# Head norms of a hybrid decoder trunk: the factor of a block by an addition and a power on GpSimd instead of five steps on ScalarE and VectorE

## The chip, the cores and the metric

The kernel runs on one core of one Trainium2 chip. The metric is the device time of one execution in microseconds. Of the kernel before there are three runs: median 1257.32 us, from 1256.88 to 1257.96. One further execution was taken with the hardware profiler; the views in this document come from it.

In the views PE is TensorE (matrix products), PEld its weight loads, DVE is VectorE, ACT is ScalarE, POOL is GpSimd and SP is SyncE, which only issues transfers. L520 is line 520 of the kernel before. Names such as s_tq are the program's tiles, with their numbers left out.

## What is computed

A trunk of two decoder layers on 512 tokens of width 1024, in float32. Layer A has sparse attention with 12 heads and memory attention with 4; layer B has dilated attention with 3 × 8 heads and memory attention with 4. Each layer ends in an MLP with a squared ReLU. Every query and key head of 64 numbers is normalised before the rotary step:

```python
def rmsnorm(x, g):
    x32 = x.astype(jnp.float32)
    y = x32 * lax.rsqrt(jnp.mean(x32 * x32, axis=-1, keepdims=True) + EPS)
    return (y * g.astype(jnp.float32)).astype(x.dtype)
...
    q = rope(rmsnorm(split_heads(q, NSA_HEADS), q_norm), pos).reshape(B, G, R, S, D)
...
    q = rope(rmsnorm(q, q_norm[:, None, None, :]), jnp.arange(S))
...
    q = rmsnorm(split_heads(q, MEM_HEADS), q_norm)
    k = rmsnorm(split_heads(k, MEM_HEADS), k_norm)
```

The scores are scaled by 64 to the power −1/2. The factor of a head is one over the root of its mean square.

## The kernel before, in words

Products of full width are made of three products of rounded halves: each float32 operand is split into a rounded high part and a low part (`wsplit` L263 and L265 for weights, `part` and `split` for activations), and `mm3` (L270 to L272) adds high × high, high × low and low × high in one PSUM bank. So every weight tile of 128 rows costs one copy on ScalarE (L263) and one subtraction on VectorE or GpSimd (L265).

The 512 tokens are four blocks of 128 rows. A projection (`proj`, L310) runs over the blocks, and in each over eight slices of the width; when a block's bank is full, a function `evac` empties it. For projections with heads it does this:

- VectorE multiplies the bank with the gains of the heads into a tile `tq` (L967 and L968 in layer A, L1487 in layer B, L632 for the memory's queries).
- `normf` (L513) makes the factor of each of the block's heads. ScalarE squares the bank (L518). VectorE sums the squares by head (L520). ScalarE then takes the logarithm of the mean square (L522), an exponential of minus half of it with the logarithm of KN in its bias (L523), and a square (L524). VectorE makes one Newton step of the result: sum plus 64 EPS times the square (L526), minus 1.5, times the first guess (L527). The sign and the constant KN are made good in the gains, which `setup2` multiplies once (L447 to L450).
- `rope` (L530) turns the heads, four steps on GpSimd (L537 to L540; VectorE takes blocks 0 and 2 of the first projection).
- `q_out` (L753) multiplies with the factor on GpSimd (L759; L1443 for the keys of layer B), splits the result into halves (L710 on ScalarE, L711 on VectorE), and, some steps of the projection later, lets TensorE transpose it (L768, L778).

`normf` is called 45 times: 12 blocks of `proj_a` and 16 of `proj_b` with six heads each, 8 of `mem_q` and 4 of `mem_out` with four, 4 of `evac_k` with eight, and once for the 96 compressed keys. Its tiles come from small rings of buffers: the sums from tag r4 with two, the three ScalarE results from r5 with two, the factors from r6 with three.

Between the projections' steps stands the attention of earlier heads: scores on TensorE, their maximum on VectorE, exponentials on ScalarE (L226), a scaling on GpSimd (`pscale`, L735), transposes (L1104, L1098, L1622), products with the values (`pair`, L747). Generators and written ratios (RA, RB, RC, DELAY, DX) say how the steps of projections, attention and side work are mixed in the program's text; the Tile framework, called with `schedule_with_timeline_sim=True`, then sets the order of each engine by a timeline that it simulates, and puts in the semaphores. Each engine works off its own queue in that order. GpSimd's queue also issues transfers that add in DRAM (L1191).

The time line of the profiled execution: projections and attention of layer A up to about 300 us, its output projection and MLP to about 670, layer B's keys, queries and attention to about 900, its output projection and MLP to the end. No head norm runs in the MLPs.

Of the kernel before, what the change touches and what calls it, by code (L numbers as in the profile page):

```python
# [10 lines left out]
AF = mybir.ActivationFunctionType  # L11
ALU = mybir.AluOpType
AX = mybir.AxisListType

P = 128
# [4 lines left out]
HD = 64  # L20
EPS = 1e-6
# [5 lines left out]

GR = ["aq", "mq0", "mq1", "bq0", "bq1", "bq2", "ak1", "ak2", "ak0", "mk0", "mk1", "kk", "b2k", "b2v"]
NQ, NK = 6, 12

KN = float(np.sqrt(0.5 / HD))


def bcast(ap, dim, n):

# [145 lines left out]
class K:  # L181
    def __init__(self, ctx, tc, ins, out):
# [13 lines left out]
        self.lab = "s"  # L196

    BUFS = dict(
        act=12, st=3, w=4, qk=8, pt4=4, p2=6, raw=2, tmp=4, sq=1, rb=1, tq=2, qki=2, ki=2, x=8, r1=1, r2=1, r3=1, r4=2, r5=2, r6=3, r7=2, nm=6, su=5, cr=6, c1=2, c2=2, nb=4,
        cs=2, stt=4, vcb=1, ab=1,  # L200
    )

# [234 lines left out]
    def setup2(self):  # L437

        nc = self.nc
        self.on1 = self.c("on1", [P, 1])  # L440
        nc.vector.memset(self.on1, 1.0)
        self.x = [None] * KT
        self.idr = self.c("idr", [P, P], F32R)
        nc.vector.tensor_copy(self.idr, self.idf)
        self.cm = self.c("cm", [P, P], F32R)
        nc.vector.tensor_copy(self.cm, self.cm0)
        for a, z, g in ((0, NQ, -(HD**-0.5) / KN), (NQ, NK, -1.0 / KN)):  # L447
            nc.vector.tensor_scalar(
                out=self.gr[:, a:z], in0=self.gr[:, a:z], scalar1=g, scalar2=None, op0=ALU.mult
            )  # L450
        self.eps = self.c("eps", [P, 3])
        for j, y in enumerate((EPS, HD * EPS, float(np.log(KN)))):
            nc.vector.memset(self.eps[:, j : j + 1], y)

    def setup_b(self):
# [57 lines left out]
    def normf(self, raw, nh, e):  # L513

        nc = self.nc
        p = raw.shape[0]
        sq = self.t("p2" if nh > 6 else "sq", [p, nh, HD])
        nc.scalar.activation(sq.rearrange("p h d -> p (h d)"), raw, AF.Square)  # L518
        ss = self.t("r4", [p, nh])
        nc.vector.tensor_reduce(out=ss, in_=sq, axis=AX.X, op=ALU.add)  # L520
        y = self.t("r5", [p, 3, nh])
        nc.scalar.activation(y[:, 0], ss, AF.Ln, scale=1.0 / HD, bias=e[:, 0:1])  # L522
        nc.scalar.activation(y[:, 1], y[:, 0], AF.Exp, scale=-0.5, bias=self.eps[0:p, 2:3])  # L523
        nc.scalar.activation(y[:, 2], y[:, 1], AF.Square)  # L524
        f = self.t("r6", [p, nh])
        nc.vector.scalar_tensor_tensor(out=f, in0=ss, scalar=e[:, 1:2], in1=y[:, 2], op0=ALU.add, op1=ALU.mult)  # L526
        nc.vector.scalar_tensor_tensor(out=f, in0=f, scalar=-1.5, in1=y[:, 1], op0=ALU.add, op1=ALU.mult)  # L527
        return f

    def rope(self, G, cs, e=None):  # L530
# [1316 lines left out]
```

## Time and profile before

| what | value |
|---|---|
| median of three runs | 1257.32 us (1256.88 to 1257.96) |
| span of the profiled execution | 1254.7 us |
| granted TensorE clock | 1.000 |
| instructions | 18245 |
| bytes moved by transfers | 215.36 MB, 172 GB/s in the mean |
| ScalarE's L522, L523, L524 together | 36.8 us in 135 instructions |
| VectorE's L526, L527 together | 34.5 us in 90 instructions |

The profiled execution's own time is its span, first to last instruction; what lies around it in a run shows in the difference to the median, 2.6 us. Busy time is the time in which an engine had at least one instruction under way; TensorE's matmuls are pipelined and their ends are modelled, so short gaps between them do not show. A row of the groups reads: line, engine, operation, output from input, shape, count, busy time and mean duration in ns of one, idle time of the engine just before them and what ended it. A row of waits reads: engine, tile and line that waited, what it waited for, us in total, times, longest.

### The profile page before, as it was taken

Reading aid. Unit: us, or ns where it says so; the run is one execution under the profiler, and the core shown is the slowest. Engines: PE = TensorE matmul, PEld = TensorE weight load, DVE = VectorE, ACT = ScalarE, POOL = GpSimd, SP = SyncE. Lnnn points to the kernel's source line nnn. Section 1 sums busy time; section 2 is a strip of 40 time slices with the busy share of each in tenths; the row PEclk is TensorE's granted clock in tenths of the full one; section 3 lists DMA queues with packets and bytes.
Section 4 is the critical chain, followed back from the end, with each engine's and each line's share of the span. In section 5 each row is a group of like instructions: output and inputs, shape, how many; then the busy total and the mean of one; then the engine's idle time right before and its main releaser. Section 6 shows DMA issues by size and latency. Waiting matters only on the chain.

```text
span 1254.7 us, 18245 instructions
## 1 busy us (share of the span) xinstructions
PE 1234.1 (98%) x6419; PEld 1018.3 (81%) x6419; DVE 831.1 (66%) x1476; ACT 744.1 (59%) x1643; POOL 341.9 (27%) x452
## 2 busy tenths in 40 slices
PE   9999999999999999999999999999999999999998
PEld 7768877787788888888888899987788888888887
DVE  6857685664576557475599477787767756557466
ACT  6835678783575454554657468778666445364462
POOL 4536874730040000000003687541232000000000
PEclk9999999999999999999999999999999999999999
DMA  7531233342497796986965431110369689697634
GB/s 267 201 106 51 94 102 124 77 111 69 160 278 227 250 257 210 276 244 203 294 205 173 137 91 47 58 39 25 113 185 306 210 267 251 204 291 225 171 104 165
DMA packets 62219, 215.36 MB, mean 172 GB/s; under 512 B 6928, under 2 KB 15312, under 8 KB 61616
## 3 DMA queue, kind: packets, MB, share of 16 engines
q1 hardware_dynamic: 50656, 143.69, 34.8%
q0 software_dynamic: 9728, 35.87, 14.7%
q10 hardware_dynamic: 1744, 34.63, 7.3%
q8 instruction: 51, 0.84, 0.3%
q14 instruction: 40, 0.33, 0.1%
HBM read 208.83 MB, written 72.35 MB: 224 GB/s over the span
## 4 chain that ended last, share of the span: by engine, by line
PE 76%; ACT 4%; DVE 4%; issue 1%; POOL 1%; DMA 0%; ACTq 0%; POOLq 0%; DVEq 0%
PE s_ps L270 13%; PE s_ps L271 13%; PE s_ps L272 13%; PE s_acc L270 5%; PE s_acc L272 5%; PE s_acc L271 5%; PE s_pt L270 3%; PE s_pt L272 3%; PE s_pt L271 3%; PE s_po L747 3%; ACT s_p L226 1%; PE s_ps L1582 1%; PE s_pt L1104 1%; PE s_ps L1069 1%; DVE s_w L265 1%
## 5 line engine op out<-in xcount | busy, mean ns | idle before, releaser
L265 DVE TENSOR_TENSOR s_w<-s_st,s_w 128x1024 fp32r<-128x1024 f32 (+3 forms) x254 | 293.6, 1160 | 250.3 <-ACT s_w L263 249.9
L263 ACT ACTIVATE s_w<-s_st 128x1024 fp32r<-128x1024 f32 (+4 forms) x260 | 251.6, 970 | 203.1 <-PE s_pt L272 58.0
L270 PE MATMUL s_ps<-s_act,s_w 128*128 128x512 f32 x560 | 218.5, 392 | 0.4 <-DVE s_x L1170 0.3
L271 PE MATMUL s_ps<-s_act,s_w 128*128 128x512 f32 x560 | 218.4, 390 | 0.0
L272 PE MATMUL s_ps<-s_act,s_w 128*128 128x512 f32 x560 | 218.1, 390 | 0.0
L1191 POOL DMA_DIRECT2D sum<-sum x16 | 14.2, 887 | 431.9 <-ACT s_p L226 431.9
L271 PEld LDWEIGHTS s_ps<-s_act,s_w 128*128 128x128 f32 x560 | 105.2, 188 | 22.5 <-issue 0.8
L270 PEld LDWEIGHTS s_ps<-s_act,s_w 128*128 128x128 f32 x560 | 105.0, 188 | 22.5 <-DVE s_x L1170 0.8
L272 PEld LDWEIGHTS s_ps<-s_act,s_w 128*128 128x128 f32 x560 | 105.2, 188 | 21.9
L270 PE MATMUL s_acc<-s_w,s_act 128*128 128x512 f32 (+3 forms) x288 | 101.2, 356 | 2.9 <-ACT s_sq L518 1.9
L271 PE MATMUL s_acc<-s_w,s_act 128*128 128x512 f32 (+3 forms) x288 | 101.1, 353 | 0.5 <-DVE s_w L265 0.5
L272 PE MATMUL s_acc<-s_w,s_act 128*128 128x512 f32 (+3 forms) x288 | 99.4, 350 | 0.0
L226 ACT ACTIVATE s_p<-s_ps 128x512 f32<-128x512 f32 x64 | 38.1, 595 | 95.0 <-PE s_ps L272 92.3
L735 POOL TENSOR_SCALAR s_p<-s_p,s_cr,s_ab 128x128 f32<-128x128 f32 (+3 forms) x96 | 61.7, 667 | 58.0 <-DVE s_cr L1080 34.8
L226 ACT ACTIVATE s_p<-s_ps,s_nm 128x256 f32<-128x256 f32 (+3 forms) x128 | 65.6, 527 | 14.1 <-DVE s_nm L726 5.0
L270 PEld LDWEIGHTS s_acc<-s_w,s_act 128*128 128x128 f32 x288 | 54.2, 188 | 9.4 <-ACT s_sq L518 3.1
L743 ACT ACTIVATE s_pt<-s_pt 128x512 f32<-128x512 f32 (+2 forms) x99 | 52.2, 532 | 14.7 <-PE s_pt L1104 5.5
L305 ACT ACTIVATE s_qk<-s_p 128x256 fp32r<-128x256 f32 (+1 forms) x96 | 46.9, 488 | 21.2 <-DVE s_p L1201 19.3
L271 PEld LDWEIGHTS s_acc<-s_w,s_act 128*128 128x128 f32 x288 | 54.3, 188 | 5.2 <-DVE s_w L265 0.9
L272 PEld LDWEIGHTS s_acc<-s_w,s_act 128*128 128x128 f32 x288 | 54.2, 189 | 4.0
L308 DVE TENSOR_TENSOR s_qk<-s_p,s_qk 128x256 fp32r<-128x256 f32 (+1 forms) x96 | 50.9, 530 | 0.0
L271 PE MATMUL s_acc<-s_w,s_qk 128*128 128x512 f32 x128 | 49.9, 390 | 0.0
(335 smaller groups left out, 2833.9 us busy)
## 6 DMA issues: line engine op xcount, KB each, us to landing
s_st<-in_w_up_dram SPq DMA_DIRECT2D x64, 512.0 KB, 4.3
s_st<-sum SPq DMA_DIRECT2D x64, 512.0 KB, 6.0
s_st<-in_w_db_dram SPq DMA_DIRECT2D x48, 512.0 KB, 4.4
sum<-in_w_db_dram POOLq DMA_DIRECT2D x16, 1024.0 KB, 14.1
sum<-sum POOLq DMA_DIRECT2D x16, 1024.0 KB, 12.0
s_st<-in_w_bq_dram SPq DMA_DIRECT2D x16, 384.0 KB, 3.2
s_st<-in_w_ag_dram SPq DMA_DIRECT2D x11, 512.0 KB, 3.6
s_w<-in_w_c_dram SPq DMA_DIRECT2D x8, 512.0 KB, 4.6
```

Of the source, the lines that this page charges most:

```text
L226: return lambda *a, **k: self.marks.append(f(*a, **k))
L263: nc.scalar.activation(w[:, 0], st, AF.Copy)
L265: e.tensor_tensor(out=w[:, 1], in0=st, in1=w[:, 0], op=ALU.subtract)
L270: mm(ps, lh[0], rh[0], start=start, stop=False, skip_group_check=again)
L271: mm(ps, lh[0], rh[1], start=False, stop=False, skip_group_check=again)
L272: mm(ps, lh[1], rh[0], start=False, stop=stop, skip_group_check=again)
L305: nc.scalar.activation(dst[:, 0], src, AF.Copy)
L308: nc.vector.tensor_tensor(out=dst[:, 1], in0=src, in1=dst[:, 0], op=ALU.subtract)
L735: self.nc.gpsimd.tensor_scalar(out=p, in0=p, scalar1=c, scalar2=g, op0=ALU.mult, op1=ALU.mult)
L743: self.turned = self.nc.scalar.activation(dst, src, AF.Copy)
L747: i = self.nc.tensor.matmul(*a, **k)
L1191: self.behind(self.nc.gpsimd.dma_start(t[o], x, accum_op=ALU.add, max_dma_last_dim=4096))
```

## The change

The factor is made from the sum of squares directly. GpSimd adds 64 EPS (times the block's mean square, as before) to the sums in place, and then raises them to the power that a constant tile holds in every element, −0.5. The three ScalarE steps, the two VectorE steps, the tag r5 and KN are gone. Since the factor is now one over the root of the sum, and no longer scaled by KN with a minus sign, the gains of the keys (columns NQ to NK of `gr`) are multiplied by 8 in `setup2`, and those of the queries by nothing: the 1/8 of the scores and the 8 of the norm cancel. The squares (L518), the sums (L520) and everything behind the factor stay as they are.

```diff
-KN = float(np.sqrt(0.5 / HD))
...
-        act=12, st=3, w=4, qk=8, pt4=4, p2=6, raw=2, tmp=4, sq=1, rb=1, tq=2, qki=2, ki=2, x=8, r1=1, r2=1, r3=1, r4=2, r5=2, r6=3, r7=2, nm=6, su=5, cr=6, c1=2, c2=2, nb=4,
+        act=12, st=3, w=4, qk=8, pt4=4, p2=6, raw=2, tmp=4, sq=1, rb=1, tq=2, qki=2, ki=2, x=8, r1=1, r2=1, r3=1, r4=2, r6=3, r7=2, nm=6, su=5, cr=6, c1=2, c2=2, nb=4,
...
-        for a, z, g in ((0, NQ, -(HD**-0.5) / KN), (NQ, NK, -1.0 / KN)):
-            nc.vector.tensor_scalar(
-                out=self.gr[:, a:z], in0=self.gr[:, a:z], scalar1=g, scalar2=None, op0=ALU.mult
-            )
-        self.eps = self.c("eps", [P, 3])
-        for j, y in enumerate((EPS, HD * EPS, float(np.log(KN)))):
+        nc.vector.tensor_scalar(
+            out=self.gr[:, NQ:NK], in0=self.gr[:, NQ:NK], scalar1=HD**0.5, scalar2=None, op0=ALU.mult
+        )
+        self.half = self.c("half", [P, 8])
+        nc.vector.memset(self.half, -0.5)
+        self.eps = self.c("eps", [P, 2])
+        for j, y in enumerate((EPS, HD * EPS)):
             nc.vector.memset(self.eps[:, j : j + 1], y)
...
         nc.vector.tensor_reduce(out=ss, in_=sq, axis=AX.X, op=ALU.add)
-        y = self.t("r5", [p, 3, nh])
-        nc.scalar.activation(y[:, 0], ss, AF.Ln, scale=1.0 / HD, bias=e[:, 0:1])
-        nc.scalar.activation(y[:, 1], y[:, 0], AF.Exp, scale=-0.5, bias=self.eps[0:p, 2:3])
-        nc.scalar.activation(y[:, 2], y[:, 1], AF.Square)
+        nc.gpsimd.tensor_scalar(out=ss, in0=ss, scalar1=e[:, 1:2], scalar2=None, op0=ALU.add)
         f = self.t("r6", [p, nh])
-        nc.vector.scalar_tensor_tensor(out=f, in0=ss, scalar=e[:, 1:2], in1=y[:, 2], op0=ALU.add, op1=ALU.mult)
-        nc.vector.scalar_tensor_tensor(out=f, in0=f, scalar=-1.5, in1=y[:, 1], op0=ALU.add, op1=ALU.mult)
+        nc.gpsimd.tensor_tensor(out=f, in0=ss, in1=self.half[0:p, 0:nh], op=ALU.pow)
         return f
```

## The prediction, made before the result

> **What bounds the kernel now.** I read the page's first part, then busy time by stretch, then the rows of the lines that change, and then what VectorE and GpSimd do around them.
>
> ```profile
> span 1254.7 us, 18245 instructions
> PE 1234.1 (98%) x6419; PEld 1018.3 (81%) x6419; DVE 831.1 (66%) x1476; ACT 744.1 (59%) x1643; POOL 341.9 (27%) x452
> ```
>
> TensorE is idle for 1254.7 − 1234.1 = 20.6 us of the span. Work taken off ScalarE or VectorE pays only where it closes such a gap, and GpSimd at 27% seems to have room. But these are averages. The next view takes six stretches in which head norms run; the view after it counts the norms in them by L527, the last step of each.
>
> ```profile
> 20.00:60.00 40.00, 37.59 (x204) 32.74 (x202) 29.53 (x73) 26.95 (x84) 24.48 (x24) 1.00 0.57 197
> 108.00:142.00 34.00, 34.00 (x204) 28.52 (x203) 26.86 (x59) 21.86 (x64) 30.99 (x46) 1.00 0.21 67
> 161.00:184.00 23.00, 22.13 (x178) 18.71 (x177) 17.59 (x44) 17.39 (x53) 20.92 (x27) 1.00 0.35 112
> 189.00:224.00 35.00, 32.86 (x261) 27.59 (x260) 21.65 (x61) 30.74 (x99) 18.13 (x28) 1.00 0.34 114
> 718.00:760.00 42.00, 39.63 (x246) 37.50 (x245) 32.62 (x56) 26.71 (x77) 34.05 (x36) 1.00 0.33 100
> 803.00:862.00 59.00, 56.72 (x440) 49.59 (x440) 46.47 (x110) 47.34 (x164) 26.92 (x32) 1.00 0.10 30
> ```
>
> ```profile
> 108.00:142.00 34.00, 3.06 (x4) 1.00 0.21 67
> 161.00:184.00 23.00, 1.02 (x2) 1.00 0.35 112
> 718.00:760.00 42.00, 3.82 (x7) 1.00 0.33 100
> ```
>
> The columns of the first are length, then busy time of PE, PEld, DVE, ACT and POOL. PE's gaps are 2.41, 0, 0.87, 2.14, 2.37 and 2.28, together 10.1 us: that is all that this change can win here, 0.8% of the time. And GpSimd is not idle where it counts: 30.99 of 34, 20.92 of 23, 34.05 of 42.
>
> What PE waits for in 718 to 760 us:
>
> ```profile
> PE s_acc L270 <- ACT s_sq L518: 1.5, 3, 0.9
> PE s_pt L768 <- DVE s_qki L711: 0.4, 1, 0.4
> PE s_acc L271 <- DVE s_w L265: 0.3, 1, 0.3
> ```
>
> All three are ScalarE or VectorE arriving late, 2.2 of the 2.37 us. None is the norm's own result: the squares (L518) empty a PSUM bank, and they stand in ScalarE's queue behind other work.
>
> **What is removed.** Each of 45 norms loses five instructions:
>
> ```profile
> L523 ACT ACTIVATE s_r<-s_r,eps x45: 281/298/393, 37.6 to 856.6; 128x6 f32<-128x6 f32 x28, 128x4 f32<-128x4 f32 x12, 128x8 f32<-128x8 f32 x4, 96x1 f32<-96x1 f32 x1
> L524 ACT ACTIVATE s_r<-s_r x45: 188/208/261, 37.9 to 857.6; 128x6 f32<-128x6 f32 x28, 128x4 f32<-128x4 f32 x12, 128x8 f32<-128x8 f32 x4, 96x1 f32<-96x1 f32 x1
> L527 DVE SCALAR_TENSOR_TENSOR s_r<-s_r,s_r x45: 149/173/1255, 39.1 to 858.1; 128x6 f32<-128x6 f32 x28, 128x4 f32<-128x4 f32 x12, 128x8 f32<-128x8 f32 x4, 96x1 f32<-96x1 f32 x1
> ...
> L522 ACT ACTIVATE s_r<-s_r,et x24: 284/300/450, 678.8 to 856.2; 128x6 f32<-128x6 f32 x16, 128x8 f32<-128x8 f32 x4, 128x4 f32<-128x4 f32 x4
> L526 DVE SCALAR_TENSOR_TENSOR s_r<-s_r,et,s_r x24: 208/227/744, 681.0 to 857.8; 128x6 f32<-128x6 f32 x16, 128x8 f32<-128x8 f32 x4, 128x4 f32<-128x4 f32 x4
> ```
>
> The three figures after the count are shortest, median and longest in ns. ScalarE: 45 × (300 + 298 + 208) = 36 us. VectorE: 45 × (227 + 173) = 18 us at the medians, but the longest are 744 and 1255, so some of them are held up; 718 to 760 us has seven L527 in 3.82 us, 546 each. In that stretch the removal takes 7 × 0.81 = 5.6 us of ScalarE's 26.71 and 3.8 + 7 × 0.23 = 5.4 of VectorE's 32.62: about a fifth and a sixth. (The 21 of L522 and L526 in the other layer are taken at the same medians.) Of three hand-offs (VectorE to ScalarE, back to VectorE, on to GpSimd) one is left, from the sum to GpSimd. And both queues lose waits at whose head these steps stood:
>
> ```profile
> POOL s_tq L759 <- DVE s_r L527: 25.0, 18, 5.3
> ...
> ACT s_r L522 <- DVE s_r L520: 10.8, 12, 2.0
> ...
> DVE s_r L526 <- ACT s_r L524: 8.0, 14, 1.2
> ```
>
> Behind L522 on ScalarE are squares, exponentials and weight copies; behind L526 on VectorE the weight splits. These 18.8 us of head-of-queue waiting end. The 25 us in which GpSimd stood at L759 for the factor are room for the two new steps.
>
> Setup loses one 128x384 multiply of the gains and keeps three small fills; TensorE is far from waiting for it, so it is put at nothing (0.36 us if it were bare):
>
> ```profile
> L448 DVE TENSOR_SCALAR gr<-gr 128x384 f32<-128x384 f32 x2 | 0.6, 360 | 0.0
> ```
>
> **What is added.** GpSimd gets 45 additions and 45 powers of at most 128x8. No power is in this trace. The nearest rows:
>
> ```profile
> L735 POOL TENSOR_SCALAR s_p<-s_p,s_cr,s_ab 128x512 f32<-128x512 f32 x24 | 20.0, 843 | 35.1 <-DVE s_cr L1080 17.6 <-PE s_acc L272 9.9 <-PE s_ps L1070 3.7
> ...
> L735 POOL TENSOR_SCALAR s_p<-s_p,s_cr,s_ab 128x128 f32<-128x128 f32 x24 | 10.9, 472 | 5.8 <-ACT s_qk L774 5.2 <-DVE s_c L1006 0.5 <-DVE s_cr L1080 0.2
> ...
> L265 POOL TENSOR_TENSOR s_w<-s_st,s_w 128x1024 fp32r<-128x1024 f32 x2 | 4.8, 2392 | 0.0
> ...
> L877 POOL MEMSET s_tmp<- 128x12 f32 x8 | 0.7, 117 | 11.3 <-PE s_acc L884 11.3
> ...
> L539 POOL TENSOR_TENSOR s_tmp<-s_tmp,s_rb 96x32 f32<-96x32 f32 x1 | 0.2, 249 | 0.1
> ```
>
> Addition: L735 has a slope of (843 − 472)/384 = 0.97 ns per element, so 0.35 us at six; at least the fill's 0.12. Power: between the fill's 0.12 and the longest elementwise instruction of this engine, 2.39. The row nearest in form is 0.25; nearest in mathematics is L522 with L523, a logarithm and an exponential, 0.60. I take 0.6: pair 0.95 us, bounds 0.24 and 2.74. A gain below nothing is excluded, since both instructions occupy the engine. GpSimd's total becomes 342 + 45 × 0.95 = 385 us.
>
> Does it fit? Room per norm is (34 − 30.99)/4 = 0.75 us in 108 to 142, (23 − 20.92)/2 = 1.04 in 161 to 184, and (42 − 34.05)/7 = 1.14 in 718 to 760. At 0.95 only the first is over, by 0.8 us, and there TensorE has no gap. Behind the addition, which waits for the sum (L520), stand the softmax scalings (L735) in layer A and the rotary steps (L537 to L540) in layer B; for those wait the transposes. One wait is new: the sum lies in a tag with two buffers, so a later L520 waits for GpSimd's power of two norms earlier, with VectorE's weight splits behind it.
>
> **VectorE and GpSimd block each other.** Same stretch, first GpSimd, then VectorE:
>
> ```profile
> 721.04 0.60 POOL L539 TENSOR_TENSOR s_tq<-s_tq,s_rb 128x192 f32<-128x192 f32 x1
> ...
> 725.83 1.34 POOL L539 TENSOR_TENSOR s_tq<-s_tq,s_rb 128x192 f32<-128x192 f32 x1
> ```
>
> ```profile
> 725.76 0.96 DVE L265 TENSOR_TENSOR s_w<-s_st,s_w 128x768 fp32r<-128x768 f32 x1 [0.22 <-ACT s_w L263]
> ```
>
> L539 takes 0.60 alone; issued 0.07 after L265 it ends at 727.17, 0.45 after L265's end at 726.72. It stood until L265 was through. So a long power would hold up the 128-row splits as well. The Trainium skill's "SBUF — State Buffer", "Who interferes with whom", states it as a rule: the pair of ports that VectorE and GpSimd share is an exclusive lock, taken by whichever starts first, and a VectorE instruction with two SBUF inputs is fully blocked by a GpSimd one that reads SBUF. These rows agree.
>
> **The sum.** Of PE's 10.1 us of gaps, ScalarE and VectorE lose a fifth and a sixth of their work and 18.8 us of blocked queue. A gap of this kind shrinks faster than the load, so I take a third, 3.3 us; a fifth gives 2.0, two thirds 6.7. Span 1254.7 − 3.3 = 1251.4. The median 1257.3 lies 2.6 us above the span, which I keep: 1254.0 us.
>
> **Rivals.** *The gaps stay and nothing moves*: for it, that PE is busy 98% and that no wait listed above is longer than 0.9 us, so a gap closed may open again at the next queued step; against it, that ScalarE's L518 alone ends 1.5 of 2.37. Time 1256.5, between 1255 and 1258. Chance 0.20.
>
> *GpSimd becomes the bound*: a pair above about 1 us fills the three dense stretches, the transposes come late, and TensorE waits. Past the room, each microsecond of the pair costs 4 + 2 + 7 = 13 us. At 1.7 us the overrun is 3.8 + 1.3 + 4.0 = 9.1, time 1266; at 2.74 it is 8.0 + 3.4 + 11.2 = 22.6, 1280. For it: a power is not in the trace and may be long; against it: six elements only. Chance 0.25.
>
> *The port rule decides*: the pair fits, but its 45 × 0.95 = 43 us of new holding stands against the two-input steps of VectorE. It decides once one in four of the 13 pairs in the three dense stretches holds up a split for which TensorE waits: 13/4 × 0.95 = 3.1 us, with no relief left, 1260.4. Against it: L526 and L527 were two-input steps themselves, and they go. The rule of the Trainium skill named above is the one at work here. Chance 0.05.
>
> *The build does not just do what the diff says*: the orders of the engines come from a timeline that the build simulates (schedule_with_timeline_sim), so its price for the power can move other work around every norm, and the gain is then lost to a worse order. One lost gap of the size of a stretch's, 2.4 us, gives 1259.7; it can as well go the other way. Chance 0.05.
>
> **Chances.** Forecast 0.45, with 1250 to 1256 as its own range. About 0.2%, 2.5 us, is what a measurement can tell from no change. Faster by more than that (below 1254.8): most of the forecast, 0.38. Within: the rest of it, nearly all of the cover case, the mildest of the GpSimd case, 0.29. Slower: 0.33. The range of 1250 to 1268 leaves out the longest powers (pairs over 1.85 us, some 0.13) and gains over 7 us (0.05).
>
> **What would show it.** ScalarE busy near 744 − 36 = 708, VectorE at most 831 − 18 = 813, GpSimd near 385. The power's row: at 0.6 or less the forecast stands; above 0.8 the dense stretches show POOL full and PE's gap in 718 to 760 growing past 2.4. L759 should wait for no VectorE step, L520's new wait should be rare, and the waits of L270 for L518 should shrink. The forecast is wrong if the power is short and PE's gaps are still 10 us.

## The result, and the profile after

The changed kernel takes 1272.76 us (median of 4 runs, 1272.08 to 1273.66), the kernel before 1257.19 us beside it (4 runs). The ratio is 1.0125, with a 95% interval of 1.0113 to 1.0137: slower by 15.6 us. The prediction was 1254.0 us with a range to 1268, so it was wrong in sign and size. What happened is its rival in which GpSimd becomes the bound, at a price above the one given there.

The head of the page of the kernel after:

```profile
span 1271.3 us, 18054 instructions
...
PE 1239.9 (98%) x6419; PEld 1026.0 (81%) x6419; DVE 813.7 (64%) x1392; ACT 717.1 (56%) x1501; POOL 417.8 (33%) x542
```

VectorE fell by 17.4 us and ScalarE by 27.0, and still the span grew by 16.6 us. GpSimd has 75.9 us more, not 43. TensorE is idle for 31.4 us in place of 20.6 (10.8 more), and its busy time for the same 6419 products is 5.8 us longer. So there are two parts: TensorE waits more, and some of its products are slower.

The new rows, grouped by form (the kernel after; busy us, then mean ns of one):

```profile
L521 POOL TENSOR_TENSOR s_r<-s_r,half 128x6 f32<-128x6 f32 x28 | 43.3, 1547 | 0.1
...
L521 POOL TENSOR_TENSOR s_r<-s_r,half 128x4 f32<-128x4 f32 x12 | 13.3, 1106 | 0.8
...
L519 POOL TENSOR_SCALAR s_r<-s_r,et 128x6 f32<-128x6 f32 x16 | 7.0, 436 | 0.0
L521 POOL TENSOR_TENSOR s_r<-s_r,half 128x8 f32<-128x8 f32 x4 | 6.7, 1665 | 0.0
...
L519 POOL TENSOR_SCALAR s_r<-s_r,ec 128x6 f32<-128x6 f32 x12 | 4.5, 377 | 5.0 <-DVE s_r L518 4.9
```

A power of six columns takes 1.55 us in the mean, where the prediction had taken 0.6. Over all 45 powers it is 63.8/45 = 1.42 us. Here are all powers and the additions of layer B (shortest, median, longest ns), by line:

```profile
L521 POOL TENSOR_TENSOR s_r<-s_r,half x45: 574/1357/2336, 38.5 to 871.2; 128x6 f32<-128x6 f32 x28, 128x4 f32<-128x4 f32 x12, 128x8 f32<-128x8 f32 x4, 96x1 f32<-96x1 f32 x1
```

```profile
L519 POOL TENSOR_SCALAR s_r<-s_r,et x24: 305/320/1286, 687.7 to 870.8; 128x6 f32<-128x6 f32 x16, 128x8 f32<-128x8 f32 x4, 128x4 f32<-128x4 f32 x4
```

The addition was sized well at the median (0.32 against 0.35); some additions take up to 1.29, so the mean is 0.40 (17.8 us over all 45). The shortest power, 574 ns, is the one of a single column (96x1); the eight-column ones take 1665. The line between them has 0.16 us per column and 0.42 in front, which gives 1.35 for six, the 1357 of the median. So the pair costs about 1.7 us per norm at the medians, 1.8 in the mean, and in the 28 norms of six columns 1.55 + 0.41 = 1.96.

Two dense stretches of the kernel after (length, busy PE, PEld, DVE, ACT, POOL, granted clock, DMA share, GB/s). They hold somewhat different work from the stretches of before, since everything is later:

```profile
718.00:760.00 42.00, 34.96 (x204) 33.77 (x202) 22.51 (x31) 15.48 (x35) 36.70 (x43) 0.96 0.40 113
760.00:803.00 43.00, 42.00 (x272) 39.23 (x273) 27.66 (x45) 30.97 (x90) 42.61 (x47) 0.96 0.20 57
```

From 718 to 760 us TensorE's gaps are 7.0 us, where they were 2.37; VectorE and ScalarE do less; GpSimd is busy 42.61 of 43 in the second stretch. And the granted clock, 1.00 in all stretches of before, is 0.96. The chain of waits from 735 to 772 us, by line, names who sets the pace:

```profile
by line: POOL s_r L521 26.2%; POOL s_rb L531 16.3%; POOL s_tq L532 15.6%; POOL s_tq L534 11.5%; POOL s_tq L533 10.5%; POOL s_tq L753 8.9%; issue 6.7%; POOL s_r L519 5.7%; POOLq L532 0.1%
```

No TensorE instruction is on it, and the power is its largest piece. GpSimd's time line there, one block of `proj_b` after another (start, length):

```profile
750.24 0.83 POOL L753 TENSOR_TENSOR s_tq<-s_tq,s_r 128x384 f32<-128x384 f32 x1
751.03 1.01 POOL L531 TENSOR_TENSOR s_rb<-s_tq,c 128x384 f32<-128x384 f32 x1
752.01 0.63 POOL L519 TENSOR_SCALAR s_r<-s_r,et 128x6 f32<-128x6 f32 x1
752.61 1.01 POOL L532 TENSOR_TENSOR s_tq<-s_tq,c 128x384 f32<-128x384 f32 x1
753.59 1.35 POOL L521 TENSOR_TENSOR s_r<-s_r,half 128x6 f32<-128x6 f32 x1
754.91 0.58 POOL L533 TENSOR_TENSOR s_tq<-s_tq,s_rb 128x192 f32<-128x192 f32 x1
755.45 0.59 POOL L534 TENSOR_TENSOR s_tq<-s_tq,s_rb 128x192 f32<-128x192 f32 x1
756.02 0.32 POOL L519 TENSOR_SCALAR s_r<-s_r,et 128x6 f32<-128x6 f32 x1
756.30 0.83 POOL L753 TENSOR_TENSOR s_tq<-s_tq,s_r 128x384 f32<-128x384 f32 x1
```

No row has an idle time in brackets: GpSimd works without a pause, and from one factor step (L753) to the next it needs 6.06 us, of which 1.35 are the power. What TensorE does at that time:

```profile
754.25 0.64 PE L762 MATMUL s_pt<-idr,s_qki 128*128 128x128 f32 x6
758.56 0.71 PE L762 MATMUL s_pt<-idr,s_qki 128*128 128x128 f32 x6 [3.67 <-DVE s_qki L705]
```

After one block's transposes it has nothing to do until the next block is through L753 (at 757.1) and VectorE's split of it (L705): a gap of 3.67 us. By name the releaser is VectorE; the engine that was late is GpSimd, one step further back. TensorE's largest waits in the whole kernel after (total us, times, longest):

```profile
PE s_pt L762 <- DVE s_qki L705: 5.5, 2, 3.7
PE s_ps L1063 <- ACT s_p L223: 3.5, 6, 1.0
PE s_ps L268 <- DVE s_w L262: 2.5, 1, 2.5
PE s_pt L1092 <- POOL s_tmp L876: 1.8, 1, 1.8
PE s_acc L267 <- ACT s_sq L516: 1.7, 3, 1.0
```

From 718 to 760 us of before, the same transposes (L768 there) waited for the split 0.4 us, once. The third row's gap shows the second part of the loss. TensorE's time line around it:

```profile
719.73 0.33 PE L269 MATMUL s_ps<-s_w,s_act 128*128 128x384 f32 x1
719.90 0.34 PE L267 MATMUL s_ps<-s_w,s_act 128*128 128x384 f32 x1
722.79 0.69 PE L268 MATMUL s_ps<-s_w,s_act 128*128 128x384 f32 x1 [2.55 <-DVE s_w L262]
723.28 0.52 PE L269 MATMUL s_ps<-s_w,s_act 128*128 128x384 f32 x1
723.60 0.52 PE L267 MATMUL s_ps<-s_w,s_act 128*128 128x384 f32 x1
...
725.84 0.39 PE L267 MATMUL s_ps<-s_w,s_act 128*128 128x384 f32 x1
726.07 0.34 PE L268 MATMUL s_ps<-s_w,s_act 128*128 128x384 f32 x1
726.24 0.34 PE L269 MATMUL s_ps<-s_w,s_act 128*128 128x384 f32 x1
```

Before the gap the same product starts every 0.17 us; after it every 0.32 us, from 723.28 until about 725.84, then every 0.17 again. So a gap of 2.55 us is followed by some 3.2 us of TensorE at half pace, which cost another 1.5 us or so. (TensorE's idle time from 756.66 to 760.07 is likewise followed by half pace, from 760.07 to 763.48.) The Trainium skill, "TensorE: Matmul & The Clock Gate", section "Part 1: The HAM clock gate", states such a gate: half the clock after an idle window of about 3.4 us, full again after about 3.4 us of work. The half pace and its length agree with these rows; the idle time ahead of it is shorter here, 2.55 us.

The length of a gap does not settle it. The kernel of experiment 11 has the same gap, and behind it the same product starts every 0.18 us at once:

```profile
725.86 0.44 PE L268 MATMUL s_ps<-s_w,s_act 128*128 128x384 f32 x1 [2.55 <-DVE s_w L262]
726.14 0.34 PE L269 MATMUL s_ps<-s_w,s_act 128*128 128x384 f32 x1
726.32 0.34 PE L267 MATMUL s_ps<-s_w,s_act 128*128 128x384 f32 x1
```

The profiled execution of the kernel after has six stretches at half clock, each 3.41 us long (a window cut to one of them shows a granted clock of 0.50); that of before has none. They begin at 56.93, 63.76, 145.68, 193.46, 722.53 and 760.07 us, so always a whole multiple of 3.413 us apart. TensorE was idle for 1.3 to 2.4 us of the 3.41 ahead of each, in several short gaps as well as in one: ahead of the first, second and fourth no gap is longer than 1.2 us. Cut at this beat, the gap of the kernel after (first two rows) lies almost whole in one stretch, that of experiment 11 (last two) is shared by two:

```profile
719.12:722.53 3.41, 1.12 (x7) 0.80 (x5) 3.41 (x5) 1.93 (x5) 3.20 (x5) 1.00 0.48 148
722.53:725.94 3.41, 3.15 (x10) 3.15 (x11) 3.40 (x5) 0.37 (x1) 3.25 (x4) 0.50 0.63 134
```

```profile
721.02:724.43 3.41, 2.29 (x13) 1.78 (x11) 3.41 (x6) 1.93 (x5) 3.23 (x6) 1.00 0.54 192
724.43:727.85 3.42, 1.99 (x11) 1.99 (x12) 3.42 (x4) 1.54 (x4) 3.26 (x4) 1.00 0.29 73
```

So what counts here looks like the idle time within one such stretch, not the length of a gap. These executions do not give a threshold: 1.77 us of idle time (753.25 to 756.66 in the kernel after) was not followed by half pace, and in an execution of experiment 3 half pace from 865.6 us came behind 0.2 us of it. The six stretches are 6 × 1.7 = 10 us of lost pace; TensorE's busy time grew by 5.8.

### The profile page after: what moved, and what is told of

Read it like the earlier page. It is cut to its first block, busy times and chain, and to the rows that moved or that the text cites. A ratio compares the mean times of both kernels' runs of the same rounds, so it can differ in the third digit from the quotient of the medians.

```text
span 1271.3 us, 18054 instructions
## 1 busy us (share of the span) xinstructions
PE 1239.9 (98%) x6419; PEld 1026.0 (81%) x6419; DVE 813.7 (64%) x1392; ACT 717.1 (56%) x1501; POOL 417.8 (33%) x542
## 4 chain that ended last, share of the span: by engine, by line
PE 81%; POOL 7%; ACT 3%; DVE 2%; issue 2%; DMA 0%; POOLq 0%; ACTq 0%; DVEq 0%
PE s_ps L267 13%; PE s_ps L268 13%; PE s_ps L269 13%; PE s_acc L267 6%; PE s_acc L268 6%; PE s_acc L269 6%; PE s_pt L269 3%; PE s_pt L268 3%; PE s_pt L267 3%; PE s_po L741 3%; POOL s_r L521 2%; ACT s_p L223 1%; PE s_ps L1063 1%; PE s_acc L878 1%; PE s_acc L573 1%
## 5 line engine op out<-in xcount | busy, mean ns | idle before, releaser
L262 DVE TENSOR_TENSOR s_w<-s_st,s_w 128x1024 fp32r<-128x1024 f32 (+3 forms) x254 | 292.9, 1156 | 257.8 <-ACT s_w L260 257.0
L521 POOL TENSOR_TENSOR s_r<-s_r,half 128x6 f32<-128x6 f32 (+3 forms) x45 | 63.8, 1418 | 0.9
L737 ACT ACTIVATE s_pt<-s_pt 128x512 f32<-128x512 f32 (+2 forms) x91 | 46.9, 519 | 17.1 <-PE s_pt L1098 8.0
L1185 POOL DMA_DIRECT2D sum<-in_w_db_dram x16 | 14.2, 890 | 116.9 <-ACT s_p L223 116.9
```

The lines of the kernel that those rows point to most:

```text
L262: e.tensor_tensor(out=w[:, 1], in0=st, in1=w[:, 0], op=ALU.subtract)
L521: nc.gpsimd.tensor_tensor(out=f, in0=ss, in1=self.half[0:p, 0:nh], op=ALU.pow)
L737: self.turned = self.nc.scalar.activation(dst, src, AF.Copy)
L1185: self.behind(self.nc.gpsimd.dma_start(t[o], x, accum_op=ALU.add, max_dma_last_dim=4096))
```

## The experiments

Theory A is the rival of the prediction: the power occupies GpSimd, whose pace sets the dense stretches. Against it stand, in the expectations, that the move itself does it, by its order and hand-offs (B), that a factor comes late in its chain of dependent steps (C), and that each power costs the same wherever it stands (D). All times are set against the kernel before on the same chip, which took 1256.2 to 1256.5 us in the four batches.

**1. A multiplication in place of the power.**

```diff
-        nc.gpsimd.tensor_tensor(out=f, in0=ss, in1=self.half[0:p, 0:nh], op=ALU.pow)
+        nc.gpsimd.tensor_tensor(out=f, in0=ss, in1=self.half[0:p, 0:nh], op=ALU.mult)
```

> The changed kernel with a multiplication in the place of the power: same engine, same operands, same count, so the factors are not those of the norm. Theory A, the length of the power on GpSimd (1.36 us in the trace after, where 0.6 was forecast): the pair shrinks from about 1.85 to about 0.6 us, GpSimd's busy time falls from 418 to about 370 us, the clock stays at 1.000, and the time is 1252 to 1258 us. Rival B, the move itself (two more entries in GpSimd's queue, the new wait of the sum's buffers, another order of the engines): the time stays above 1265 us.

Measured 1259.67 us (7 runs), ratio 1.003 (1.0018 to 1.0042), 1.7 us above A's range, at a clock of 0.994 to 0.999. The row that changed, in this kernel's groups:

```profile
L521 POOL TENSOR_TENSOR s_r<-s_r,half 128x6 f32<-128x6 f32 x28 | 9.1, 326 | 0.2
```

With the same instructions in the same places but 0.33 us in place of 1.55, most of the loss is gone: of 1.25% (15.6 us), 0.95% or 12 us go with the power's length. Per norm that is 1.1 us shorter on average, so 11 us for each, near the 13 of the prediction's rival. The build orders the engines anew here too, as it does in every experiment. The other 3.2 us over the kernel before are taken up in 3 and 10.

**2. The power beside the five steps, unread.** To the kernel before, an addition and a power on GpSimd are added in each norm, and the factor is made as before.

```diff
+        g = self.t("r8", [p, nh])
+        nc.gpsimd.tensor_scalar(out=g, in0=ss, scalar1=e[:, 1:2], scalar2=None, op0=ALU.add)
+        nc.gpsimd.tensor_tensor(out=g, in0=g, in1=self.half[0:p, 0:nh], op=ALU.pow)
```

> The kernel before with its factor made as before, and behind each norm the addition and the power on GpSimd as well, into a tile that nobody reads. Theory A, GpSimd occupied: nobody waits for the power, but the rotary steps and scalings behind it in the queue come later all the same, so most of the loss is there: 1268 to 1278 us, clock below 1.000. Rival C, the length of the dependent chain from the sum to the factor: that chain is as before, so the time is 1257 to 1260 us.

Measured 1279.79 us (4 runs, 1275.51 to 1281.42), ratio 1.0179 (1.0158 to 1.02). No step waits for this power's result, and it costs 23.3 us, a little over A's range. C falls as the main cause: what costs is GpSimd's time, not the factor's way through the chain.

**3. The factor by ScalarE alone.** A logarithm and an exponential, without Newton's step, without GpSimd.

```diff
-        nc.gpsimd.tensor_scalar(out=ss, in0=ss, scalar1=e[:, 1:2], scalar2=None, op0=ALU.add)
+        nc.scalar.activation(ss, ss, AF.Ln, bias=e[:, 1:2])
         f = self.t("r6", [p, nh])
-        nc.gpsimd.tensor_tensor(out=f, in0=ss, in1=self.half[0:p, 0:nh], op=ALU.pow)
+        nc.scalar.activation(f, ss, AF.Exp, scale=-0.5)
```

> The factor from two ScalarE steps alone, a logarithm of the sum and an exponential of minus half of it; no Newton step on VectorE, nothing on GpSimd, so the factor is as fine as ScalarE's two tables are. It tells what the relief is worth that the prediction put at 3.3 us: one ScalarE and two VectorE steps of each norm gone and no cost on GpSimd. If the relief closes gaps of TensorE as forecast: 1251 to 1256 us. If the gaps stay (the rival of the prediction in which nothing moves): 1256 to 1258 us.

> The factor by ScalarE's logarithm and exponential alone, once more and with more rounds beside the kernel before: nothing of it on GpSimd, and two VectorE steps and one ScalarE step per norm fewer. It was 1.3 us (0.1%) under the kernel before; the relief of ScalarE and VectorE expects 0 to 3 us under it, 1253 to 1256 us, and no difference if VectorE's and ScalarE's steps had slack.

Measured 1255.21 us (10 runs), ratio 0.9991 (0.9982 to 1.0), and in a later batch 1254.80 us (11 runs), ratio 0.9992 (0.9983 to 1.0001). Here GpSimd's load stays as in the kernel before and three of the five steps go. That is worth 1 to 1.5 us, at the edge of what the runs tell from nothing. The prediction had put the relief by all five at 3.3 us; no run takes all five away without giving GpSimd the pair.

**4. The power only where GpSimd has room.** In the 13 norms of `mem_q`, `mem_out` and the compressed keys the power, in the 32 others the five steps of before; the constants of the gains follow. Experiments 5, 6 and 7 use the same switch in other calls of `normf`.

```diff
-    def normf(self, raw, nh, e):
+    def normf(self, raw, nh, e, power=False):
...
+        if power:
+            nc.gpsimd.tensor_scalar(out=ss, in0=ss, scalar1=e[:, 1:2], scalar2=None, op0=ALU.add)
+            f = self.t("r6", [p, nh])
+            nc.gpsimd.tensor_tensor(out=f, in0=ss, in1=self.half[0:p, 0:nh], op=ALU.pow)
+            return f
...
-        f = self.normf(ps[:, 0:256], 4, e[:, b])
+        f = self.normf(ps[:, 0:256], 4, e[:, b], True)
```

> The power only in the 13 norms of mem_q, mem_out and the compressed keys, which mostly fall outside GpSimd's dense stretches; the other 32 as before. Theory A with room as the condition: nothing lost, 1255 to 1259 us, clock 1.000. Rival D, every power costs its share wherever it stands (15.6 us / 45 = 0.35 us each): 1261 to 1263 us.

Measured 1256.30 us (10 runs), ratio 1.0002 (0.9992 to 1.0011). The powers there are not short:

```profile
L526 POOL TENSOR_TENSOR s_r<-s_r,half 128x4 f32<-128x4 f32 x12 | 12.5, 1041 | 1.0
```

Thirteen powers, 12 of them 1.04 us long, cost nothing that can be measured. D falls: it is the place that decides.

**5 and 6. The power only in `proj_a` (12 norms), and only in `proj_b` with the keys of layer B (20 norms).**

> The power only in the 12 norms of proj_a (layer A, six heads); the other 33 as before. Theory A, GpSimd's room in the dense stretches: in the trace before the room was 3.0 us for the four norms of 108 to 142 us and 2.1 for the two of 161 to 184; at a pair of 1.85 us these are overrun by 4.4 and 1.6 us, and the slowed clock behind the gaps comes on top: 1261 to 1266 us. Rival D, the same share for every norm: 12 x 0.35 = 4.2, 1260.7 us. If layer B carries all: 1257.

> The power only in the 20 norms of layer B's queries and shared keys (proj_b, evac_k); the other 25 as before. Theory A: seven norms in the dense stretch of 718 to 760 us overrun its room by 5.0 us, the four of the keys come late too, and the clock: 1263 to 1268 us; with the run that has the power in proj_a alone and the one that has it in the 13 sparse norms it adds up to the 15.6 us of the change within 3 us. Rival D, the same share for every norm: 20 x 0.35 = 7.0, 1263.5 us, so this run alone does not tell it from theory A; the three together do. If layer A carries all: 1257.

Measured 1268.15 us (ratio 1.0091, 1.0076 to 1.0106) and 1268.95 us (1.0102, 1.0084 to 1.0119), four runs each: 12.0 and 12.8 us, both above A's ranges (the second by 1 us). The first rotation of layer B's keys on GpSimd stands between the two layers; its start (before "to") dates that point. In the kernel before, then in 5, then in 6:

```profile
L537 POOL TENSOR_TENSOR s_rb<-s_x,c x8: 733/739/979, 676.3 to 703.7; 128x256 f32<-128x256 f32 x8
```

```profile
L544 POOL TENSOR_TENSOR s_rb<-s_x,c x8: 732/738/987, 688.4 to 715.8; 128x256 f32<-128x256 f32 x8
```

```profile
L544 POOL TENSOR_TENSOR s_rb<-s_x,c x8: 728/748/991, 676.3 to 712.7; 128x256 f32<-128x256 f32 x8
```

In 5 that point is 12.1 us late and nothing is lost behind it; in 6 it is not late at all and all is lost behind it. So each dense stretch pays for its own powers. In the kernel after, where the first rotation starts at 685.1, layer A loses 8.8 us and the rest 16.6 − 8.8 = 7.8. The two halves add up to 24.8 us, 9 more than the whole, where the expectation had them meet it within 3 us. Equal shares of 0.35 us for every norm (D) would have been 4.2 and 7.0.

**7. Both halves, and the five steps in the 13 sparse norms.** The scale constants of some gains are not those of the norm here.

> The power in the norms of proj_a, of proj_b and of the key side together, and the five steps of the kernel before in the 13 sparse norms (mem_q, mem_out, compressed keys), so that it differs from the changed kernel only there. If the cost of a stretch is its own, the two halves alone (+12.0 and +12.8 us) add up to 1280 to 1282 us. If the halves alone pay for something that the whole does not (the order of the instructions around them, or the sparse norms' relief), the time is near the changed kernel's 1272.

Measured 1278.68 us (4 runs), ratio 1.0177 (1.0163 to 1.0191): 22.3 us, 1.3 us below the range for the sum of the halves, and 0.5% (6.5 us) slower than the change, although GpSimd has 13 powers fewer. The next two were made for this.

**8. The five steps back beside the pair, unread:** in the 13 sparse norms (first), in all 45 (second). The addition writes the factor's tile, so that the sums stay as they are.

```diff
-        nc.gpsimd.tensor_scalar(out=ss, in0=ss, scalar1=e[:, 1:2], scalar2=None, op0=ALU.add)
...
+        nc.gpsimd.tensor_scalar(out=f, in0=ss, scalar1=e[:, 1:2], scalar2=None, op0=ALU.add)
+        nc.gpsimd.tensor_tensor(out=f, in0=f, in1=self.half[0:p, 0:nh], op=ALU.pow)
+        if idle:
+            y = self.t("r5", [p, 3, nh])
+            nc.scalar.activation(y[:, 0], ss, AF.Ln, scale=1.0 / HD, bias=e[:, 0:1])
+            nc.scalar.activation(y[:, 1], y[:, 0], AF.Exp, scale=-0.5, bias=self.eps[0:p, 2:3])
+            nc.scalar.activation(y[:, 2], y[:, 1], AF.Square)
+            g = self.t("r8", [p, nh])
+            nc.vector.scalar_tensor_tensor(out=g, in0=ss, scalar=e[:, 1:2], in1=y[:, 2], op0=ALU.add, op1=ALU.mult)
+            nc.vector.scalar_tensor_tensor(out=g, in0=g, scalar=-1.5, in1=y[:, 1], op0=ALU.add, op1=ALU.mult)
```

> The changed kernel, and beside the pair the five steps of the kernel before into tiles that nothing reads, in the 13 sparse norms alone. If the load of these steps on ScalarE and VectorE is what makes the power in the dense norms alone 6.7 us slower than the change, the time is 4 to 8 us over the changed kernel, 1276 to 1281 us. If it is the order or the latency of the sparse factors, it stays within 2 us of it, 1270 to 1274.

> The same with the five unread steps in all 45 norms: the engines then do what they do in the kernel before with an unread power (1279.8 us), but the factor comes from the power. If the load of ScalarE and VectorE sets the difference of that kernel to the changed one, 1278 to 1282 us; if only the factor's lateness or the order does, 1271 to 1275.

Measured 1276.73 us (ratio 1.0158, 1.0144 to 1.0173) and 1276.98 us (1.0167, 1.0149 to 1.0185), four runs each: 4.1 and 5.3 us over the change by the ratios. The 13 sparse norms' steps alone cost most of the 6.5 us; those of the 32 dense norms add nothing that these runs tell. The second is between its two ranges. So steps on ScalarE and VectorE seem to be worth more once GpSimd is late: 1 to 1.5 us for three of the five without the pair (3), 4 to 5 for the five with it. Why the sparse norms and not the dense ones, and how much the build's order has in it, stays open.

**9. Twice the buffers for sums and factors** (r4 from 2 to 4, r6 from 3 to 6): no sum waits for an earlier power.

> The changed kernel with four buffers for the sums and six for the factors in place of two and three, so that VectorE's sum never waits for a power of two norms before. If that wait carries part of the loss, 1265 to 1270 us; by theory A, where GpSimd's own length sets the pace, it is as the changed kernel, 1271 to 1275.

Measured 1273.85 us (4 runs), ratio 1.0133 (1.0116 to 1.0151), the same as the change. The new wait that the prediction named carries none of the loss that these runs can tell, and in the trace of the change no sum (L518) waits for a power at all.

**10. GpSimd's pair at other lengths.** To the kernel before, an unread addition and multiplication (as in 2, with `mult`); to the kernel after, a second, unread power:

```diff
+        g = self.t("r8", [p, nh])
+        nc.gpsimd.tensor_tensor(out=g, in0=ss, in1=self.half[0:p, 0:nh], op=ALU.pow)
```

> The kernel before with an addition and a multiplication on GpSimd per norm into a tile that nothing reads: some 0.6 us per norm in place of the 1.75 us of the addition and the power. Theory A with a room of 0.75 to 1.14 us per norm in the dense stretches expects 0 to 3 us over the kernel before, 1256 to 1260 us. A theory that any two instructions more on GpSimd cost their length times their number on the path (45 x 0.6 us, of which two thirds in the dense stretches) expects 18 us, 1274 us; a value between 1260 and 1270 would say that the rooms are about half of those read from the windows.

> The changed kernel with a second power per norm into a tile that nothing reads, right behind the first: GpSimd's work per norm rises by another 1.4 us (the mean of the power in the changed kernel). Theory A (GpSimd's pace sets the end of the stretches where rooms are 0.75 to 1.14 us per norm, 10 to 13 us of time for each us per norm beyond the room) expects 14 to 18 us over the changed kernel, 1286 to 1292 us, with GpSimd at about 480 us. Theory C (a late factor of a fixed delay, or the order alone) expects at most 1280, as a factor comes no later than before; a lengthening past 1295 would say that a us of GpSimd costs more the more there is of it.

Measured 1264.66 us (4 runs, 1260.78 to 1266.73), ratio 1.0061 (1.0044 to 1.0078), and 1299.01 us (4 runs), ratio 1.0336 (1.0322 to 1.0351). Both are above A's numbers. Unread work on the kernel before, 0.6 to 0.8 us per norm, costs 8.3 us, where rooms of 0.75 to 1.14 should have hidden nearly all; in effect the rooms are smaller than the idle time, if it is GpSimd's time that costs. (The execution at a clock of 0.999, in the table below, still has 4.4 us of it.) A second power, 1.32 us in the mean, costs another 26 us, 20 for each us, where A had 10 to 13; so a microsecond of GpSimd costs more the more there is of it. In that kernel from 770 to 780 us:

```profile
770.00:780.00 10.00, 6.36 (x27) 6.11 (x26) 4.45 (x8) 5.60 (x14) 9.84 (x13) 0.66 0.00 0
```

GpSimd is busy 9.84 of 10, TensorE 6.36, and at a granted clock of 0.66. Its wait of the transposes for the split is

```profile
PE s_pt L764 <- DVE s_qki L707: 10.3, 7, 3.6
```

seven gaps where the change had two. Part of the excess may be the clock, which A did not contain. Executions of one and the same program give an idea of its size:

| kernel | time us at granted clock, one execution each |
|---|---|
| 10, unread multiplication | 1260.78 at 0.999; 1263.67 and 1265.64 at 0.996; 1266.73 at 0.993 |
| 2, unread power | 1275.51 at 0.993; 1278.27 at 0.989; 1281.31 and 1281.42 at 0.987 |

Nothing in the program differs within a row of this table, and 0.006 of clock go with 6 us. The kernel after runs at 0.992 to 0.995, the second power at 0.981 to 0.985, the kernel before at 0.998 to 1.000. At 1 us for each 0.001 that would be some 6 us of the change's 15.6, an estimate; the change's own four executions (1273.66 at 0.992, 1272.08 at 0.995) have half that slope. It is a relation between executions, in which longer gaps can lengthen the time and lower the clock at once, not a run with the clock held at 1.00.

**11. TensorE kept busy in a gap.** The kernel already issues unused products in one such place (`keep`); here 13 of them fill the gap of 3.67 us behind the transposes of an early block of `proj_b`.

```diff
-                self.keep(self.last, 3)
+                self.keep(self.last, 3 if b == NB - 1 else 13)
...
-            return kept if sp == 0 and b == NB - 1 else turn
+            return kept if sp == 0 and b >= NB - 2 else turn
```

> The changed kernel with 13 more products whose result nobody uses, put into TensorE's order in the one gap of 3.67 us that the trace after shows at 755 us, behind the transposes that end ahead of it. They need 13 x 0.22 = 2.9 us and so fit into the gap; the order of all else is the same. If the slow clock after a gap (0.83 in 760 to 770 us, 384-column products 0.32 us apart instead of 0.17) is the gap's consequence, the clock of that stretch goes to 1.00 and the time falls by about 1.6 us, to 1270 to 1272. If the slow clock has another cause, the time is 1272 to 1274 us and the clock row stays.

Measured 1273.42 us (4 runs), ratio 1.0134 (1.0118 to 1.0151): nothing is won, and the time is in the range that was given for another cause of the slow clock. Three stretches of this kernel:

```profile
750.00:760.00 10.00, 9.64 (x58) 8.65 (x57) 3.22 (x5) 3.89 (x10) 9.92 (x13) 1.00 0.01 2
760.00:770.00 10.00, 6.92 (x42) 6.54 (x43) 7.74 (x13) 7.20 (x18) 9.84 (x10) 0.94 0.35 116
770.00:780.00 10.00, 9.74 (x52) 9.22 (x51) 6.25 (x13) 5.46 (x16) 9.92 (x13) 0.72 0.14 43
```

The first gap is filled and no slow stretch follows it at once, but 3 us of gaps open in the next 10 us, and the clock of 0.72 comes behind those. So the slow clock moved with the idle time; that idle time is its only cause is not shown (see the gap of 2.55 us above). As GpSimd is busy for 9.92, 9.84 and 9.92 of 10, a TensorE that ran faster would mostly have waited longer.

**12. Other work off GpSimd.** In every second block of `proj_b` the rotary steps go to VectorE.

```diff
-            self.rope(t, self.cs[:, b])
+            self.rope(t, self.cs[:, b], nc.vector if b % 2 == 0 else nc.gpsimd)
```

> The changed kernel, with the rotary steps of every second block of proj_b on VectorE: 8 x 3.7 us of other work leave GpSimd, the power stays. Theory A, GpSimd full: the gaps of layer B shrink, 1264 to 1269 us, and a clock nearer to 1. Rival C, the latency of addition and power in the chain from the sum to the factor: that chain is untouched, 1271 to 1275 us.

Measured 1269.67 us (4 runs), ratio 1.0112 (1.0097 to 1.0127): some 1.6 us less than the change by the ratios, just outside A's range, and the intervals overlap. Layer A is untouched by it: in its trace the first rotation of layer B's keys starts at 685.5 us, as late as in the change. Behind that point its span of 1266.7 us loses 12.0 − 9.2 = 2.8 us to the kernel before, where the change loses 7.8, and no slow stretch is left there. That is the way that A says, but it is one execution, the fastest of the four.

**13. The version to which this points:** ScalarE's pair (3) in the 32 dense norms, the power in the 13 sparse ones.

> ScalarE's logarithm and exponential in the 32 dense norms, GpSimd's addition and power in the 13 sparse ones: GpSimd as in the kernel with the sparse power (about 360 us), ScalarE some 8 us below that with the pair everywhere. By the sum of the two runs, 1.2 us under the kernel before from ScalarE's pair and nothing from the sparse power: 1253 to 1257 us. A loss of over 2 us would say that a sparse power is not free once its neighbours changed.

Measured 1256.70 us (11 runs), ratio 1.0 (0.9991 to 1.0009). No gain; of all these, ScalarE's pair everywhere is the best, at 0.1% under the kernel before.

## Why the prediction was wrong

**The step that failed** is the one beginning "Power: between the fill's 0.12 and the longest elementwise instruction of this engine, 2.39", which ends in "I take 0.6". It took the price of ScalarE's logarithm and exponential for GpSimd. The power is 1.42 us in the mean, inside the bounds but far from the value taken, and even its part in front, 0.42 us, is above the 0.25 of the row nearest in form. In the 28 norms of six columns the pair is 1.96 us, twice the 0.95 of the sum. All that followed ("at 0.95 only the first is over") hung on it.

**The rival had the mechanism, and its price was too low.** It gave 13 us for each us past the room, and 1266 at a pair of 1.7. Experiment 1 measures 11 for each, and 2, 4, 5 and 6 show that it is GpSimd's time in the dense stretches that costs. At the measured 1.96 its formula gives 4 × 1.21 + 2 × 0.92 + 7 × 0.82 = 12.4 us, 6.7 for layer A and 5.7 for layer B; the halves alone cost 12.0 and 12.8. Its three stretches hold 13 of the 32 norms that 5 and 6 move. That the whole, 15.6, comes near to it is in part luck. Its chance of 0.25 was too low: the bounds of the pair ran from 0.24 to 2.74 and the rooms end near 1, so most of what was not excluded lay on the rival's side.

**A term was missing:** the granted clock. The prediction read 1.00 in every stretch and let it stand. In the kernel after six stretches of 3.41 us run at half pace, behind others in which TensorE stood idle for 1.3 to 2.4 us. How much of the 15.6 us is theirs no run separates; the table in 10 puts it at some 6. The range held pairs up to 1.85 us; the pair of six columns is beyond that, at 1.96.

**The rooms were read too large.** Idle time of an engine in a stretch counted as room for each norm. Experiment 10 finds a cost at 0.6 to 0.8 us already. A likely reason, not shown, is that idle time that stands between two waits takes up only part of the new work.

**The relief is not shown at the 3.3 us forecast:** 3, which takes away three of the five steps, gains 1 to 1.5. ScalarE lost 27.0 us where 36 were forecast; VectorE 17.4 where 18 were, which is luck: the two steps had taken 34.5 us, and other work came to VectorE, such as seven more copies of transposed blocks (24 before, 31 after).

**What held:** the addition's 0.35 (0.32 at the median); setup at nothing (TensorE's first wait, for a fill of `eps`, is 1.2 us before and after, though the prediction called it far from waiting); the new wait for a sum's buffer, called rare (9); and the lock between VectorE and GpSimd as not what decides. It is there; first VectorE, then GpSimd, in the kernel after:

```profile
763.70 1.13 DVE L262 TENSOR_TENSOR s_w<-s_st,s_w 128x768 fp32r<-128x768 f32 x1 [2.19 <-ACT s_w L260]
```

```profile
763.98 2.07 POOL L521 TENSOR_TENSOR s_r<-s_r,half 128x6 f32<-128x6 f32 x1
```

L262 ends at 764.83, and 1.36 (an undisturbed power) later it is 766.19; the power ends at 766.05. So it seems to have stood until VectorE was nearly through. In this direction the lock lengthens some powers; the mean at six columns is 1.55. L262's own mean is 1156 ns where it was 1160, so VectorE's splits are not held up more than before.

## What to carry to other kernels

Where no row of the trace has an operation, the nearest in mathematics on another engine is no price for it: run it alone once, or weigh the whole span between the bounds. Before work is given to an engine at 27% of the span, see what it has left in the stretches where the work will stand, and do not count all of its idle time there as room. And where TensorE's idle time grows, look at the granted clock as well as at the gaps: here six times 1.3 to 2.4 us of it within 3.41 us, often in several short gaps, were followed by 3.41 us at half pace.

## What was not expected of the hardware

A GpSimd power of 128x6 takes 1.36 us undisturbed, four times a multiplication of the same shape (0.33), and grows by 0.16 us for each column from 0.57 at one. TensorE fell to half pace for 3.41 us behind a gap of 2.55 us in one kernel and not behind the same gap in another, and all six slow stretches of one execution begin whole multiples of 3.413 us apart. And the time of one program moved with the granted clock by 6 us between executions (0.999 to 0.993) where it had such stretches, while the kernel before kept to 0.998 to 1.000.
